# Ten staged batches instead of eight, four DMAs per direct batch, and a last batch stored without spilling, in a sliding-window copy

## The chip, the cores and the metric

One core of a Trainium2 chip runs the kernel. A *call* below is one session of measurements; the calls of the experiments ran on chips 0, 2 and 15. The time is the device time of one execution in microseconds (us); medians over several executions are quoted, and a ratio is the mean time of one kernel's fast runs over that of the other's fast runs of the same rounds, so it is not quite the ratio of the medians. Below 1 is faster. All runs used here were in the fast state, at a granted clock of 1.0; one of the 19 executions of run 7 was slow (785.26 us) and is left out.

## The reference

```python
batch, length, dim = (32, 4096, 256)          # float32
window_size, stride = 64, 32
n_windows = (length - window_size) // stride + 1   # 127
for i in range(n_windows):
    start = i * stride
    result[:, i] = x[:, start:start + window_size]
```

Each window is 64 x 256 floats, 64 KiB, contiguous in input and output. Neighbouring windows share half their rows. A "block" below is 32 rows (32 KiB): a batch has 128 blocks, window w is blocks w and w+1, and a batch has 127 windows.

## The kernel before

It only moves data, on two queues. A *direct* batch goes from HBM to HBM on the sync queue (q1 in the profile), each window one run of 64 KiB. A *staged* batch is loaded once into SBUF as 128 rows of one block, then stored twice, once as the first half and once as the second half of the windows, on the scalar queue (q10). Staging reads the input once instead of twice but passes more bytes through the DMA engines (100.66/8 = 12.6 MB a batch on q10, 199.76/24 = 8.3 MB on q1).

```python
def windows(self, q, b, w0, n):            # direct: n windows of batch b
    blk = self.blk
    self.count(q.dma_start(
        out=self.oap((b * self.nw + w0) * 2 * blk, [[2 * blk, n], [1, 2 * blk]]),
        in_=self.xap(b * self.nb + w0, [[blk, n], [1, 2 * blk]]),
        max_dma_last_dim=65536))

def store(self, q, t, b, half):            # staged: all 128 blocks as one half
    w = b * self.nw - half
    return q.dma_start(
        out=self.oap(w * 2 * blk + half * blk, [[2 * blk, self.nb], [1, blk]]),
        in_=t[:, :])
# ... (Staging.run: load ahead in 4 buffers, store half 0, store half 1)
staged = list(range(1, B, 4))              # 8 batches
# ...
    w0 = 1 if b - 1 in staged else 0
    w1 = last if b + 1 in staged else n_win
    c.windows(ring_d, b, w0, 112)
    c.windows(ring_d, b, w0 + 112, w1 - w0 - 112)
for g in range(n_st - 1):
    st.wait_stored(ring_d, g)
c.shared_of(ring_d, 0, 4, n_st - 1, last)  # small copies, 16 parts of 4 KiB a window
c.shared_of(ring_d, 2, 4, n_st - 1, 0)
st.wait_stored(ring_d, n_st - 1)
c.shared(ring_d, staged[-1] - 1, last, 1)
c.shared(ring_d, staged[-1] + 1, 0, 1)
```

128 blocks stored as halves of 127 windows *spill* one half window into the batch before and one into the batch after. The neighbours therefore leave those windows out of their direct copies, and small copies mend them once the store is done.

## Time and profile before

| | before |
|---|---|
| median of the first three runs | 775.56 us |
| span of the profiled run | 775.2 us |
| DMA packets, traffic through the engines | 7536, 300.42 MB |
| last packet of q10 (staged) | 720 us |
| last packet of q1 (direct) | 773.5 us |
| a window between 10 and 600 us | 2.62 us |
| a staged row (32 KiB) between 10 and 600 us | 1.33 us |

The median is that of the recorded runs, the span and the packets are on the page, and the last four lines are from the records of single packets in the trace. Columns of the windows view are: stretch, its length, busy time of each compute engine with its count, granted clock, DMA share (mean busy share of 16 DMA engines) and GB/s they moved. A byte copied between HBM and HBM counts once in GB/s but twice in HBM traffic (on the page: 233.31 MB read and 266.86 MB written, together 500.17; 2 x 199.76 of q1 + 100.66 of q10 = 500.18). The lines themselves are in the prediction.

### The profile page before, as it was taken

How to read it: one execution, taken by the hardware profiler on the slowest of the kernel's cores; microseconds unless marked ns; L12 is line 12 of the kernel's file. 1: busy time of each engine (PE TensorE's matmuls, PEld its weight loads, DVE VectorE, ACT ScalarE, POOL GpSimd, SP SyncE). 2: the span in 40 equal slices, each digit the busy share in tenths (PEclk: the TensorE clock that was granted, in tenths of full speed). 3: DMA queues.
4: the chain of work that ended last, by engine and by line, in shares of the span. 5: the costliest groups of instructions: out<-in, count | busy, mean ns of one | idle time of the engine just before them, and what ended most of it. 6: DMA issues, size and time to landing. Idle time of an engine off the chain costs nothing. (4 is left out here: it accounts for less than half of the span.)

```text
span 775.2 us, 129 instructions
## 1 busy us (share of the span) xinstructions
POOL 0.2 (0%) x4
## 2 busy tenths in 40 slices
POOL 0000000000000000000000000000000000000000
DMA  9999999999999999999999999999999999999984
GB/s 375 367 429 387 391 406 401 391 404 397 413 386 386 413 396 402 387 392 419 386 408 375 413 408 386 404 394 408 401 394 413 375 413 397 402 406 357 316 327 180
DMA packets 7536, 300.42 MB, mean 388 GB/s; under 512 B 1176, under 2 KB 1176, under 8 KB 1432
## 3 DMA queue, kind: packets, MB, share of 16 engines
q1 hardware_dynamic: 4080, 199.76, 65.0%
q10 hardware_dynamic: 3456, 100.66, 32.9%
HBM read 233.31 MB, written 266.86 MB: 645 GB/s over the span
## 5 line engine op out<-in xcount | busy, mean ns | idle before, releaser
L172 POOL MEMSET const-bfloat16-1.0<- 128x1 bf16 x1 | 0.1, 102 | 0.0
L172 POOL MEMSET const-uint8-127<- 128x1 uint8 x1 | 0.1, 101 | 0.0
L172 POOL MEMSET const-float32-0.0<- 128x1 f32 x1 | 0.1, 99 | 0.2 <-issue 0.2
L172 POOL MEMSET const-float32-1.0<- 128x1 f32 x1 | 0.1, 98 | 0.0
## 6 DMA issues: line engine op xcount, KB each, us to landing
out_dram<-xb_58 ACTq DMA_DIRECT2D x4, 4096.0 KB, 153.8
out_dram<-xb_59 ACTq DMA_DIRECT2D x4, 4096.0 KB, 170.0
out_dram<-xb_60 ACTq DMA_DIRECT2D x4, 4096.0 KB, 163.8
out_dram<-xb_61 ACTq DMA_DIRECT2D x4, 4096.0 KB, 156.5
xb_58<-in_x_dram ACTq DMA_DIRECT2D x2, 4096.0 KB, 62.9
xb_59<-in_x_dram ACTq DMA_DIRECT2D x2, 4096.0 KB, 93.7
xb_60<-in_x_dram ACTq DMA_DIRECT2D x2, 4096.0 KB, 109.7
xb_61<-in_x_dram ACTq DMA_DIRECT2D x2, 4096.0 KB, 123.7
```

The costliest lines, as they stand in the source:

```text
L172: nc = _bacc.Bacc("TRN2", target_bir_lowering=False, num_devices=1)
```

## The change

The intent: take 2 more batches off the HBM-to-HBM path, give the staged queue a larger part of each engine so both queues end together, and avoid a wait at the very end.

```diff
-    def store(self, q, t, b, half):
+    def store(self, q, t, b, half, p0=0, n=None):
...
+        if g == len(self.batches) - 1:
+            for half, p0, rows in ((0, 0, 112), (0, 112, 15), (1, 1, 15), (1, 16, 112)):
+                self.c.count(self.c.store(q, self.tiles[i], self.batches[g], half, p0, rows))
+            return
...
-    staged = list(range(1, B, 4))
+    staged = list(range(1, B - 3, 3))
...
-            c.windows(ring_d, b, w0, 112)
-            c.windows(ring_d, b, w0 + 112, w1 - w0 - 112)
+            for n in (32, 32, 48, w1 - w0 - 112):
+                c.windows(ring_d, b, w0, n)
+                w0 += n
...
-        st.wait_stored(ring_d, n_st - 1)
-        c.shared(ring_d, staged[-1] - 1, last, 1)
-        c.shared(ring_d, staged[-1] + 1, 0, 1)
```

(Cut to its core; the small copies also change their step from 4 to 3.)

More of the change, by code (lines that the diff above doesn't have):

```diff
@@ L65, in load @@
         )
-    def store(self, q, t, b, half):
+    def store(self, q, t, b, half, p0=0, n=None):
         blk = self.blk
-        w = b * self.nw - half
+        n = self.nb if n is None else n
+        w = b * self.nw + p0 - half
         return q.dma_start(
-            out=self.oap(w * 2 * blk + half * blk, [[2 * blk, self.nb], [1, blk]]),
-            in_=t[:, :],
+            out=self.oap(w * 2 * blk + half * blk, [[2 * blk, n], [1, blk]]),
+            in_=t[p0 : p0 + n, :],
         )
@@ L135 @@
     ring_d, ring_s = nc.sync, nc.scalar
+    spilled = staged[:-1]
     with tc.tile_critical():
@@ L142 @@
                 continue
-            w0 = 1 if b - 1 in staged else 0
-            w1 = last if b + 1 in staged else n_win
-            c.windows(ring_d, b, w0, 112)
-            c.windows(ring_d, b, w0 + 112, w1 - w0 - 112)
-        for g in range(n_st - 1):
-            st.wait_stored(ring_d, g)
-        c.shared_of(ring_d, 0, 4, n_st - 1, last)
-        c.shared_of(ring_d, 2, 4, n_st - 1, 0)
-        st.wait_stored(ring_d, n_st - 1)
-        c.shared(ring_d, staged[-1] - 1, last, 1)
-        c.shared(ring_d, staged[-1] + 1, 0, 1)
+            w0 = 1 if b - 1 in spilled else 0
+            w1 = last if b + 1 in spilled else n_win
+            for n in (32, 32, 48, w1 - w0 - 112):
+                c.windows(ring_d, b, w0, n)
+                w0 += n
+        for g in range(len(spilled)):
+            st.wait_stored(ring_d, g)
+        c.shared_of(ring_d, 0, 3, len(spilled), last)
+        c.shared_of(ring_d, 2, 3, len(spilled), 0)
         ring_d.wait_ge(c.done, c.total)
```

## The prediction

> **What bounds the kernel now.** No compute engine works here: the kernel only copies. So I read, in this order, the page's slices and queue rows, then the table of windows, then the sync queue's own waits, and last the records of single DMA packets, which the trace holds (queue, start, duration, bytes).
>
> The page first. The DMA engines are busy from the first slice to the last but one, so what counts is their work and its rate; only the last four slices fall off.
>
> ```profile
> span 775.2 us, 129 instructions
> ...
> DMA  9999999999999999999999999999999999999984
> GB/s 375 367 429 387 391 406 401 391 404 397 413 386 386 413 396 402 387 392 419 386 408 375 413 408 386 404 394 408 401 394 413 375 413 397 402 406 357 316 327 180
> ...
> q1 hardware_dynamic: 4080, 199.76, 65.0%
> q10 hardware_dynamic: 3456, 100.66, 32.9%
> HBM read 233.31 MB, written 266.86 MB: 645 GB/s over the span
> ```
>
> q1 is the sync queue (24 direct batches, HBM to HBM), q10 the scalar queue (8 staged batches: one load, two stores each). Together they take 97.9% of the 16 engines. A direct batch is 199.76/24 = 8.3 MB of engine traffic and twice that in HBM traffic; a staged one is 100.66/8 = 12.6 MB of each.
>
> The windows show two regimes and an unfilled end.
>
> ```profile
> 200.00:400.00 200.00, 0.00 (x0) 1.00 1.00 399
> ...
> 680.00:692.00 12.00, 0.00 (x0) 1.00 1.01 434
> ...
> 710.00:750.00 40.00, 0.00 (x0) 1.00 0.90 323
> 750.00:760.00 10.00, 0.00 (x0) 1.00 0.77 306
> 760.00:775.00 15.00, 0.00 (x0) 1.00 0.35 150
> ```
>
> The last two columns are the DMA share and GB/s. While both queues run the rate is 399. From 710 on only direct copies are left, the share is 0.90 and the rate 323: the last q10 packet ends at 720 us, the last q1 packet at 773.5. The sync queue's waits say the same: it waits for staged batches only to issue a few small copies, and then waits 51 us for the direct copies.
>
> ```profile
> SPq L102 <- DMA out_dram<-xb_60: 55.7, 1, 55.7
> SPq L137 <- DMA out_dram<-in_x_dram: 51.0, 1, 51.0
> SPq L56 <- DMA out_dram<-xb_61: 39.6, 1, 39.6
> ```
>
> The chain of waits on the page holds 0.5 us of constants and follows no DMA, so it carries nothing here.
>
> **The turns, from the packet records.** Between 10 and 690 us q1 ran 3299 packets and q10 3303; in stretches of 20 us, 79 and 79, 108 and 108, 86 and 84. An engine takes one packet of each queue in turn, and the 4-byte semaphore packets (about 0.01 us) count as turns. A q1 packet is a window of 64 KiB, a q10 packet a row of 32 KiB. Before, one engine's turns for a direct batch are 7 windows + 1 semaphore, then 1 window + 1 semaphore: 8 data in 10. For a staged batch they are three times 8 rows + 1 semaphore: 24 in 27. That gives 0.8 x 64 : 0.889 x 32 = 1.80 : 1; the rates between 10 and 690 us are 257 and 142 GB/s, 1.82 : 1. So the number of DMAs, through their semaphores, decides how the queues share an engine.
>
> [...] 112 windows use 16 engines, but the remainders of 14 or 15 use 14 or 15. The 792 semaphore packets on q1 are exactly 24x16 + 16x14 + 8x15 + 4x16, and the share of 0.90 after 710 us is about 14 of 16 engines. [...]the shortest 64 KiB packet took 2.418 us, 27.1 GB/s per engine or 434 in all, and the 434 of the window 680 to 692 reaches it.[...]
>
> **The path that sets the end.** Fourteen engines have the full load: 24x8 = 192 windows and 192 rows. The one without remainders has 168 windows. From the records, a window takes 2.62 us on average up to 700 us and 2.85 us after 702, when q10 is gone; a row takes 1.33 us. Full engine before: q10 needs 8x27 = 216 turns, in which q1 gets 216x0.8 = 172.8 windows: 172.8x2.62 + 192x1.33 = 453 + 255 = 708 us. The remaining 19.2 windows at 2.85 are 55 us. With 16 small packets of 0.17 us (3 us) and the first packet at 2 us that is 768. The span is 775, so 7 us are not in this sum[...]. I carry these 7 over.
>
> **The change, part by part.**
> Two more staged batches, two fewer direct ones. A full engine loses 2x8 windows, 16x2.62 = 42 us, and gains two times 24 rows, 48x1.33 = 64 us: +22 us if packets keep their times. HBM traffic goes the other way. q1 carries 14x176 + 158 + 154 = 2776 windows, 181.9 MB, plus 1.2 MB of small copies; q10 carries 125.8 MB. HBM: 2x183.1 + 125.8 = 492 MB against 500, -1.6%. Engine traffic: 309 MB against 300, +2.8%.
>
> Four DMAs for a direct batch. The same bytes on the same engines (2+2+3 windows, then the remainder), but 12 turns for 8 windows. Ratio 0.667x64 : 0.889x32 = 1.5 : 1. The 44 more semaphores per engine cost about 0.5 us at 0.01 us each. Their use is the balance: q1 needs 22x12 = 264 turns, plus 20 for the small copies; q10 needs 9x27 + 9 + 20 = 272. Both queues end together, and the 55 us of direct copies alone, at 2.85 instead of 2.62, vanish: 19.2x0.23 = -4 us.
>
> The last staged batch without spill. The two late single-window copies that wait for it go. The remaining small copies wait for the ninth staged batch, done about 20 q10 turns before the end, so their short packets alternate with the last stores. Before, the packets after 760 us ran at 150 GB/s; perhaps 3 us of this end is saved.
>
> Packets kept at their old times (all load on engines): 176x2.62 + 240x1.33 + 3 + 2 + 7 = 461 + 319 + 12 = 792, less 3 for the end and a few more because the two lightly loaded engines finish early: 786 to 790.
>
> Packets made faster because HBM limits them: this is the step I have to judge. For it: direct copies alone, on 14 engines, moved 323 GB/s, 646 in HBM, with windows stretched to 2.85, so fewer engines did not go faster. The mixed phase moved 257x2 + 142 = 656 in HBM at 2.62. A fit over 20 us stretches between 10 and 690 us gives 2.84 us per MB of q1 and 1.91 per MB of q10, a ratio of 1.5, where pure engine limits give 1 and pure HBM limits 2. With it, after is 183.1x2.84 + 125.8x1.91 = 520 + 240 = 760; before gives 759 by the same sum, and took 775, that is 16 more (start, end, two idle engines, the slow direct phase). Of these 16 about 4 go with the direct phase and 3 with the end: 760 + 9 = 769. If HBM alone held at 656, 492/656 = 750, and 750 + 9 = 759.
>
> **The rivals.**
> 1. Engines are the limit, not HBM: 786 to 790. For it: packets follow each other within some ns and a fifth of the windows between 400 and 600 us run at their shortest time. Against: the typical window is 8% above its shortest, and slower still where q10 was absent.
> 2. HBM is the whole limit: about 759. For it: 434 GB/s in the one stretch where q10's part was larger (about 44%). Against: the fit's 1.5 rather than 2, and that stretch is 12 us.
> 3. Scattering: with 32 windows in a DMA the engines stand 2 windows apart, 128 KiB of output, where they stood 7 apart. [...] Nothing in the trace before speaks for it, as no DMA there has such a pitch on q1.
> 4. Balance missed: if turns are not strictly alternate, one queue ends late. Twenty turns off would be some 20x1.33 = 27 us of one queue alone, but at fuller packet speed than with both, so only some 5 us net: 775. Against it stand the equal packet counts.
>
> **Range and chances.** The middle way gives 769; I take 768, a little nearer to HBM for the 434 stretch. Rival 2 puts the lower edge at 756, rival 1 the upper at 786. The bounds of 2% are 760 and 791. Faster by more needs HBM as the whole limit: 0.19. Slower by more needs rival 1 and rival 3 at once: 0.05. Within: 0.76.
>
> **What would show each step.** Balance: q10's last packet within 10 us of q1's, and q1 at about 1.5 times q10's rate. Turns: 1400 semaphore packets on q1 and 510 on q10. Relief of HBM: mixed rate 403 to 410 rather than 399, windows at 2.57 rather than 2.62. End: no stretch of 40 us at 323. I am wrong if the rate stays at 399 or below (rival 1, or 3 where windows are above 2.62), or if one queue still runs alone for 40 us.

## The result, and the profile after

The changed kernel took 767.8 us (median of 4, 766.7 to 770.8); the kernel before, in the same rounds and the first three runs, 777.4 (median of 4). The ratio of the means over all of these is 0.9884, 95% interval 0.9836 to 0.9933: faster, by less than 2%.

From the page of the changed kernel: slices, queues, HBM.

```profile
span 767.1 us, 176 instructions
...
GB/s 357 393 402 417 417 414 403 412 415 414 390 415 425 407 402 402 431 410 402 396 427 415 402 397 425 407 407 400 431 405 403 396 429 407 427 429 407 401 364 208
...
q1 hardware_dynamic: 4464, 183.11, 57.9%
q10 hardware_dynamic: 4348, 125.77, 40.4%
q14 instruction: 1, 0.01, 0.0%
HBM read 225.05 MB, written 266.93 MB: 641 GB/s over the span
```

The engines moved 8.5 MB more than before, HBM 8.2 MB less (read 233.31 before), and the long drop of the last four slices is now two. The windows view of the changed kernel:

```profile
200.00:400.00 200.00, 0.00 (x0) 1.00 1.00 410
...
680.00:700.00 20.00, 0.00 (x0) 1.00 1.01 423
700.00:720.00 20.00, 0.00 (x0) 1.00 0.95 402
720.00:740.00 20.00, 0.00 (x0) 1.00 0.90 382
740.00:760.00 20.00, 0.00 (x0) 1.00 0.80 326
760.00:780.00 20.00, 0.00 (x0) 1.00 0.03 14
```

The mixed phase, in which both queues run, is at 410 instead of 399 GB/s. No stretch of direct copies alone is left: at a DMA share of 0.90 the rate is 382 where it was 323. The sync queue's waits (SPq is its sequencer, xb the staging tiles) show the same:

```profile
SPq L108 <- DMA out_dram<-xb: 160.3, 3, 61.6
SPq L144 <- DMA out_dram<-in_x_dram: 46.5, 1, 46.5
```

Three waits for staged batches (before the small copies), one for the end; the wait for a staged batch that stood alone before the two late copies (39.6 us before) has gone. That does not yet say that it cost anything.

From the packet records of both kernels, packets that start between 10 and 600 us; HBM is 2 x q1 + q10:

| | before | after |
|---|---|---|
| packets of q1 and q10 | 2867 and 2860 | 3302 and 3293 |
| GB/s of q1 and q10 | 257 and 141 | 246 and 163 |
| HBM GB/s | 656 | 655 |
| window, row | 2.62, 1.33 us | 2.55, 1.30 us |
| windows at their shortest time (under 2.45 us) | 31% | 47% |
| last window, last row | 771, 720 us | 753, 763 us |

HBM ran at the same rate in both kernels (656 and 655 GB/s) while the engines' rate, both queues together, rose by 2.6% (398.4 to 408.6 GB/s). That is the reading on which the rest stands.

### The profile page after: what moved, and what is told of

Same layout as the page of the kernel before. It is cut to its first block, busy times and chain, and to the rows that moved or that the text cites. A ratio compares the mean times of both kernels' runs of the same rounds, so it can differ in the third digit from the quotient of the medians.

```text
span 767.1 us, 176 instructions
## 1 busy us (share of the span) xinstructions
POOL 0.2 (0%) x4
```

## The experiments

My theory before them: the two queues take turns on each engine, packet by packet, semaphore packets included, so the number of DMAs sets the mix; the mix sets HBM bytes per engine byte; and HBM, at a fixed rate (656 and 655 GB/s above), sets the speed of the mixed phase. The turns are read from the records between 10 and 600 us. They name no engine, but 5691 times before the change and 6643 times after it a packet began 3 or 4 ns before another one's end, and in 99.4% and 98.6% of these cases the two were of different queues (48% and 47% at distances of some 50 ns). The counts agree only with the semaphore packets, of about 0.01 us each, included: without them, q1 and q10 ran 2317 and 2542 before, 2220 and 2927 after. Rivals: the engines themselves are the limit; the staged batches do it alone; splitting helps in some other way (distance between engines); the end does it.

One caution for all comparisons. The kernel before ran at 767.5 and 767.8 us in the two calls of the first eight runs below, but at 777 to 778 in the calls of the result and of the last four. The third run below, whose mix is that of before, shows why in its records: 2 x 261 + 143 = 665 GB/s of HBM in the mixed phase where the kernel before had 656. HBM was 1.4% faster there, whatever the reason; it was not the chip, as chip 2 served both a call at 767.8 and one at 778.3 us. So each ratio is taken within its call, and times of different calls are not compared. The expectations of runs 1 to 8 give absolute times too, reckoned from 775 us; for these the ratios are what is judged.

**1. Staged batches and end, without the split**

```diff
-            for n in (32, 32, 48, w1 - w0 - 112):
+            for n in (112, w1 - w0 - 112):
```

> 10 staged batches and the last one without spill, but each direct batch in 2 DMAs as before. Theory (turns and HBM): 10 turns for 8 windows, so q1 has 220 turns and q10 272; the direct copies end first, near 725 us, and q10 runs on alone for about 45 rows at its shortest time, 1.22 us: 776 to 784 us, mixed rate back at 398 to 400 GB/s, ratio to before about 1.00 to 1.01. Rival (the two more staged batches do it by sparing HBM, the split does nothing): about 768, ratio 0.99.

Measured: 790.3 us, ratio 1.0284 (1.0248 to 1.032): slower than the 1.00 to 1.01 expected, and far from the rival's 0.99. The turns came out: q1 260 and q10 143 GB/s, as before the change, in spite of 10 staged batches; the last window ended at 719 us and q10 ran on alone. But it ran on slowly:

```profile
730.00:740.00 10.00, 0.00 (x0) 1.00 0.88 380
740.00:780.00 40.00, 0.00 (x0) 1.00 0.79 260
```

In the same trace, rows started after the last window and before 741 us took 1.25 us on average, those after it 1.62: 57% of these ran at the shortest time, the others took up to 4 us. From about there on q10 is in the last batch, stored in pieces of 112 and 15 rows. Run 10 follows this up. What follows here: two more staged batches alone do not make the gain.

**2. The split alone**

```diff
-            c.windows(ring_d, b, w0, 112)
-            c.windows(ring_d, b, w0 + 112, w1 - w0 - 112)
+            for n in (32, 32, 48, w1 - w0 - 112):
+                c.windows(ring_d, b, w0, n)
+                w0 += n
```

> The kernel before with each direct batch in 4 DMAs and nothing else. Theory: the turns give q10 40%, the mixed rate rises to 410 GB/s, q10 ends near 620 us and 48 windows of each full engine are left to run alone at 3 us or so: 772 to 782, ratio to before about 1.00 (the HBM bytes are the same 500 MB). Rival (splitting itself makes direct copies faster): below 768 with windows faster than 2.85 when alone.

Measured: ratio 1.0007 (0.9993 to 1.0021), 768.3 us. The windows view:

```profile
200.00:600.00 400.00, 0.00 (x0) 1.00 1.00 416
640.00:700.00 60.00, 0.00 (x0) 1.00 0.98 324
```

q10 ended at 627 us (expected 620) and left direct copies alone for some 136 us, at first at 324 GB/s, 648 in HBM. Windows took 2.97 us on average from 640 us on, so the rival (faster than 2.85) fails. The mixed phase was faster (416) by about what the direct phase then gave back: the HBM bytes are those of before. Splitting by itself was worth nothing here; it only moved bytes between two phases that HBM limits nearly alike (665 and 648 GB/s).

**3. The end alone** (the edit in words, against the kernel before)

```diff
+        if g == len(self.batches) - 1:   # four pieces, no spill, as in the change
...
-    staged[-1]'s two late single-window copies
```

> The kernel before with the last staged batch stored in four pieces without spill, and nothing else. Theory: the two late single-window copies go, 0 to 4 us: 772 to 777, ratio 0.995 to 1.0. Rival (the late copies are the larger part of the gain): 768 or less.

Measured: ratio 0.998 (0.9965 to 0.9995), 766.2 us. Some 1.5 us. The time lies under the rival's 768, but so does that of the kernel before in this call (767.5); the ratio decides against the rival.

**4. The same number of turns, other distances**

```diff
-            for n in (32, 32, 48, w1 - w0 - 112):
+            for n in (80, 16, 16, w1 - w0 - 112):
```

> The changed kernel with the 4 DMAs cut 80, 16, 16 and the rest instead of 32, 32, 48 and the rest: the same number of turns, other distances between the engines (5 windows, then 1). Theory: as the changed kernel, ratio 0.985 to 0.992, mixed rate 408 to 412. Rival (distance between the engines matters): a mixed rate off by 2% or more.

Measured: 763.6 us, ratio 0.9943 (0.9926 to 0.996), mixed rate 411 to 412 GB/s. The rate is as expected; the ratio missed the range narrowly. The changed kernel itself was not in this call, in which the kernel before took 767.5 us and HBM moved 660 GB/s in this run's mixed phase, so whether the smaller gain belongs to this split or to the call stays open. The distance between the engines (worked out as if each took its windows in a row; the records name no engine) shows no loss in the rate.

**5. More HBM bytes, same packets**

```diff
-            in_=t[p0 : p0 + n, :],
+            in_=self.xap(b * self.nb + p0, [[blk, n], [1, blk]]), max_dma_last_dim=65536,
```

The staged stores read HBM; loads and everything else stay, and the result is still right.

> The changed kernel with the staged stores reading their rows from HBM instead of SBUF (loads kept, result still right): the same packets and turns, HBM traffic 492 + 84 = 576 MB. HBM theory: 655 GB/s again, packets longer by a sixth, mixed rate about 350 GB/s, 880 to 900 us. Engine theory: 768 and 410 GB/s.

Measured: 881.8 us. Where q10 only stores, every packet of both queues goes between HBM and HBM; from the windows view:

```profile
740.00:800.00 60.00, 0.00 (x0) 1.00 0.99 330
```

330 is 660 in HBM, read and written. The kernel before took 767.8 us in this call, and the changed kernel 767.8 in that of the result: the same sequence of packets on the same engines took 114 us longer with 84 MB more for HBM to move. Reading from HBM is not slow by itself: the 28 rows left after the last window took 1.21 us, the shortest time. So HBM, or the path to it, which no run here tells apart, limits the mixed phase; a limit of the engines would have left the time alone.

**6. Fewer HBM bytes, same packets** (a wrong result on purpose)

```diff
-                in_=self.xap(b * self.nb + w0, [[blk, n], [1, 2 * blk]]),
+                in_=self.src[:n, :],       # constant tile, 112 rows of 64 KiB
```

> The changed kernel with the direct copies reading a constant SBUF tile instead of HBM (result wrong on purpose; the direct queue starts some 10 us late): the same packets and turns, HBM traffic 492 - 182 = 310 MB. HBM theory: nothing stretches the packets, windows at 2.42 to 2.45, mixed rate 430 or more, about 725 to 740 us. Engine theory: windows at 2.54, 410 GB/s, 768 or more.

Measured: 1575.8 us, a mean window of 5.43 us, 216 GB/s between 200 and 600 us. It answers nothing about HBM: it put another limit in its place, and what that is I did not test. The 216 is the rate of both queues; the windows alone, 64 KiB in 5.43 us on 16 engines, come to 193 GB/s.

**7 and 8. More staged batches, with turns to match**

```diff
-    staged = list(range(1, B - 3, 3))
+    staged = list(range(1, B, 3))                       # run 7: 11
-            for n in (32, 32, 48, w1 - w0 - 112):
+            for n in (32, 32, 32, 16, w1 - w0 - 112):
```
```diff
+    staged = list(range(1, B - 3, 3)) + [30, 31]        # run 8: 12, two without spill
+            for n in (16,) * 7 + (w1 - w0 - 112,):
```

> 11 staged batches, direct batches in 5 DMAs (13 turns for 8 windows: 273 + 22 on q1 against 299 on q10). HBM theory: 487 MB, mixed rate near 417, 757 to 763 us, ratio to before 0.975 to 0.983. Engine theory: 13 us more than the changed kernel per further staged batch at most, 775 to 780.

> 12 staged batches (the last two without spill), direct batches in 8 DMAs (16 turns for 8 windows: 320 + 22 on q1 against 328 on q10). HBM theory: 483 MB, mixed rate 425 to 432, close to the shortest packets; 744 to 754 us, ratio 0.96 to 0.97. Engine theory: 780 or more. Rival: with pieces of 16 windows neighbouring engines read overlapping rows; if that costs, windows stay above 2.5 and the gain is lost.

Measured: ratios 1.0064 (1.0044 to 1.0084) and 1.0001 (0.9986 to 1.0016). Both missed, and run 8 fell between the two theories. The mixed rates were near those expected (419 GB/s for 417, and 424 for 425 to 432), and windows in run 8 took 2.48 us, so its rival (above 2.5) is not seen. The windows view of run 8:

```profile
200.00:600.00 400.00, 0.00 (x0) 1.00 1.00 424
720.00:760.00 40.00, 0.00 (x0) 1.00 0.84 344
```

What I left out was the fully loaded engine. With the mean packet times of each run, its sum is 176 x 2.54 + 240 x 1.29 = 757 us for 10 staged batches (the changed kernel), 168 x 2.50 + 264 x 1.28 = 758 for 11, and 160 x 2.48 + 288 x 1.25 = 757 for 12. No window or row in any trace was shorter than 2.415 and 1.211 us. At these times the sums would be 716, 725 and 736 us: each further staged batch adds 24 rows for 8 windows, some 10 us, and leaves less that a relief of HBM can shorten. In run 8 82% of the windows were already at their shortest time, and HBM was down to 648 GB/s. Why the other 18% were still stretched there is not shown. Rows in odd pieces are a part of both misses: the last two batches of run 8 took 1.33 us a row, the rows that ran alone in run 7 1.56. Run 7 also missed its balance: I had counted the 22 short turns of the small copies (0.16 us each in the changed kernel) as if they filled time, so its windows ended at 732 us and rows ran on alone to 766.

**9. The changed kernel again** (no edit)

> The changed kernel once more, unaltered, beside the two below, because the second chip runs the kernel before about 1.3% faster than the first one did. If the gain is a matter of HBM bytes and turns, the ratio to before on the same chip is 0.985 to 0.995 here too, with a mixed rate 2 to 3% above that of before. If it were an accident of one chip, the ratio would be 1.0.

Measured: 768.7 us against 778.3, ratio 0.9877 (0.985 to 0.9904), mixed rate 409. The gain repeats. (The expectation puts the difference of the calls down to another chip; the records speak against it, as said above. The gain has been repeated only in calls where the kernel before took 777 to 778 us.)

**10. Staged batches alone, with spill and two DMAs**

```diff
-    staged = list(range(1, B, 4))
+    staged = list(range(1, B - 3, 3))
```

> 10 staged batches, 2 DMAs per direct batch, and the last staged batch with spill as before: the first run of the series with its last batch back in rows of 128. There the rows, once alone, took 1.5 to 1.9 us instead of 1.22, in pieces of 112 and 15 rows. Theory A (the pieces of 112 and 15 rows are slow when stores run alone): rows alone at 1.21 to 1.3 us, ratio to before 1.01 to 1.02. Theory B (any stores alone are slow): rows alone at 1.5 us or more, ratio 1.025 to 1.035.

Measured: ratio 1.0101 (1.0072 to 1.013). Rows alone, in the windows view:

```profile
730.00:760.00 30.00, 0.00 (x0) 1.00 0.89 385
```

All 594 rows that started after the last window took 1.21 us on average, where those of run 1 after 741 us took 1.62: theory A. Stores in rows of 128 ran at their shortest time when alone; stores in pieces of 112 and 15 rows did not. No run here shows why.

**11. Equal load on all 16 engines**

```diff
-            for n in (32, 32, 48, w1 - w0 - 112):
+            rest.append((b, w0 + 112, w1 - w0 - 112))
+            for n in (32, 32, 16, 16, 16):
                 c.windows(ring_d, b, w0, n)
                 w0 += n
+        for b, w0, n in rest:
+            c.shared(ring_d, b, w0, n)
```

> The changed kernel with the remainders of 14 and 15 windows taken out of the stream and copied at the end in 16 parts of 4 KiB per window, so that all 16 engines have the same load; the other 112 windows in 5 DMAs (12 turns as in the changed kernel for 7 windows). If HBM limits while all engines are busy: mixed rate about 420, then 20 MB in small packets at 320 to 330 GB/s on 16 engines, 748 to 758 us, ratio 0.975 to 0.988. If packets of 4 KiB between HBM and HBM are slow in bulk (0.25 us or more each): 765 or more.

Measured: 767.1 us, ratio 0.9857 (0.9828 to 0.9885). Better than the changed kernel by less than the intervals can tell, and not the 748 to 758 expected, though the ratio lies in its range of 0.975 to 0.988.

```profile
200.00:600.00 400.00, 0.00 (x0) 1.00 1.00 418
700.00:750.00 50.00, 0.00 (x0) 1.00 1.02 326
```

The engines were full to about 750 us, at 326 GB/s or 652 in HBM when only small direct copies were left; these took 0.20 us each, less than the 0.25 of the rival. So with idle engines removed, HBM accounts for nearly the whole time: 492 MB / 654 GB/s = 752 us, plus start and end, for a span of 764.5. My expectation had left out 1.2 MB of small copies and too much of start and end.

**12. The change without its third part** (the edit in words)

```diff
-        if g == len(self.batches) - 1:   # four pieces, no spill
+        # last staged batch stored as all others; two late single-window copies
```

> The changed kernel without its third part: 10 staged batches and 4 DMAs per direct batch, but the last staged batch stored with spill as before, with the two late single-window copies behind it. This completes the table of parts: split alone gave a ratio to before of 1.001, the end alone 0.998, the staged batches alone 1.010. Theory (the two first parts only pay together, the third is worth some us at most): rows at the end at 1.21 us, late copies 2 to 4 us behind the last store, ratio 0.985 to 0.995. Rival (the third part carries the gain): ratio 1.0 or more.

Measured: 767.5 us, ratio 0.987 (0.9842 to 0.9897), the same as run 9. Rows after 750 us took 1.21 us here, and 1.36 to 1.42 in the two traces of the changed kernel. The last row ended at 760 us and the late copies 3 us later; in run 9 the last row ended at 763. So what the late copies cost is about what the odd pieces cost.

The parts together, each against the kernel before in its own call:

| staged | DMAs per direct batch | end | ratio | kernel before in that call, us |
|---|---|---|---|---|
| 8 | 4 | spill | 1.0007 | 767.5 |
| 8 | 2 | no spill | 0.998 | 767.5 |
| 10 | 2 | no spill | 1.0284 | 767.5 |
| 10 | 4 (80, 16, 16 and rest) | no spill | 0.9943 | 767.5 |
| 10 | 2 | spill | 1.0101 | 778.3 |
| 10 | 4 | spill | 0.987 | 777.0 |
| 10 | 4 | no spill (the change) | 0.9877 | 778.3 |

Neither of the first two parts helped alone; together they are the gain. Two limits: the split alone was run only where HBM was faster, and the size of the gain does not carry over, with 0.6% there (with another split) and 1.2 to 1.3% elsewhere. No version clearly beat the changed kernel.

## Why the prediction was right

It said 768 us and within 2%; measured were 767.8 and 0.9884.

- **Turns.** Right to the packet: 1400 semaphore packets on q1 and 510 on q10, equal packet counts in the mixed phase (3302 and 3293), rates 246 to 163 = 1.51 to 1 where 1.5 was worked out. Run 1 with the old turns kept the old rates although it staged 10 batches, and run 2 with the new turns got the new ones with 8.
- **Balance.** Right: the last packets of the queues lie 2 us apart (763.5 and 765.5), and the 8 turns more of q10 show as windows ending at 753 and rows at 763.
- **Engine against HBM.** I chose the middle between a pure engine limit (786 to 790) and a pure HBM limit (759). For the mixed phase the pure HBM limit was the better description: 656 and 655 GB/s before and after, and run 5 at 660 with other bytes. The rate, 409 to 410, was at the upper end of my 403 to 410. The fit with its ratio of 1.5 understated the relief: its 760 us of mixed work would be 308.9 MB / 410 = 753. The trace did not determine that ratio: done again on it (bytes of a packet spread over its duration), the fit gives 1.5 for 20 us stretches from 10 us on, 1.7 when they begin 5 us later, and 1.7 to 2.5 for stretches of 40 us. So the middle way rested on the choice of stretches.
- **What lies outside the mixed phase.** Here I was off the other way: 9 us allowed, 767 - 753 = 14 measured. The term mis-sized is the end. From 700 us on, the engines with no remainders run dry, and 14 full engines are left (the DMA share is 0.90 between 720 and 740 us, 14.4 of 16). Their windows take 2.44 to 2.54 us, near the shortest time, and HBM moves 628 GB/s between 700 and 740 us, so it hardly limits them: 14 engines at 27.1 GB/s are 379, and the view shows 382. In run 12, without the odd pieces, windows and rows after 700 us took 2.42 and 1.21 us. The two errors, 7 and 5 us, nearly cancel, so the exact hit is partly luck. It is luck too that the result fell in a call with the HBM rate of the trace before: in the call of run 4 the kernel before took 767.5 us to begin with.
- **The third part.** I gave it 3 us. Alone it was worth 1.5 (run 3), and within the change nothing that can be seen (runs 9 and 12): by run 12 its odd pieces cost about what the late copies did. With rows left to run alone it was a loss (run 1 against run 10).
- **Rival 3, the distances.** That they might cost time was a guess; no trace had shown it. No loss appeared: the mixed rate with pieces of 32 (run 2) and of 80 and 16 (run 4) is what the mix and HBM give.

## What to carry to other kernels

When two DMA queues share the engines, count packets per queue, semaphores included: the number of DMAs acted as a weight here (257 and 141 GB/s with two to a direct batch, 246 and 163 with four), and two queues of unlike work could be made to end together with it. When copies go between HBM and HBM, do the sum in HBM bytes, read plus written, as well as in engine bytes, and beside both the sum of the fullest engine; none of the runs went below the largest of the three (for the changed kernel 492 MB at 655 GB/s of HBM, 751 us; 308.9 MB at the 434 GB/s of the shortest packets, 712; and 716 for the fullest engine; its span was 767), and a change that lowered one soon met the next. A part that does nothing alone may still be half of a gain, so try the parts in pairs before dropping one.
